# FFN up-projections by Strassen block products over both token halves, all of them ahead of the down-projections

## The chip, the cores and the metric

The kernel runs on one core of a Trainium2 chip. What is measured is the device time of one execution in microseconds (us), the median of several runs. The engines are named as in the profile: PE is the matrix engine (PEld its weight loads), DVE the vector engine, ACT the scalar engine, POOL GpSimd, and SP the engine whose queue issues nearly all DMAs. A matmul's result lies in a bank of PSUM; everything else lies in SBUF or in the chip's DRAM.

## The reference, cut to what matters

One block of a hybrid attention model on 1024 tokens with 1024 channels. The change touches the last line alone, the feed-forward part with its causal convolution of width 3 along the tokens:

```python
def _conv_ffn(h, w_up, conv_w, w_down):
    u = h @ w_up                                   # 1024 x 1024 @ 1024 x 5632
    u = lax.conv_general_dilated(u, conv_w[:, None, :], window_strides=(1,),
                                 padding=((CONV_WIDTH - 1, 0),), ...)
    a, b = jnp.split(u, 2, axis=-1)
    return (jax.nn.silu(a) * b) @ w_down           # 1024 x 2816 @ 2816 x 1024
...
        x = x + y @ w_out[l]
        x = x + _conv_ffn(_rms_norm(x, norm_ffn[l]), ffn_up[l], ffn_conv[l], ffn_down[l])
```

All of it is in float32, and the kernel keeps that accuracy: every matrix and every activation is split into a high part and a remainder ("hi" and "lo", e.g. whi and wlo), and one product is made of three matmuls, whi·xhi, whi·xlo and wlo·xhi, added in one PSUM bank.

## The kernel before

Channels lie on the 128 partitions, tokens along the free axis, in two halves h=0 and h=1 of 512. The 5632 up channels are 44 groups of 128; the gate pairs group i (o=0, called a) with group 22+i (o=1, called b), so that there are 22 **pairs** i. One up-projection of one group for one half is 8 k-tiles times 3 = 24 matmuls of a 128x128 weight tile by 128x512 tokens (`mm3`).

A weight group arrives by a DMA of 512 KB on SP's queue (`wraw`), ACT makes its hi part (L217), POOL its lo part (L218). The results are consumed from PSUM: ACT copies with the tap's factor (L1263), DVE adds the two other taps (L1267, which read PSUM and u) and the two leading tokens from the previous half (L1271: `prev`, 1 and 2 columns wide); ACT takes the tanh (L1278), DVE forms silu times gate (L1279, L1280), ACT and POOL split that into hh and hl (L1283, L1284).

Before the stretch of the change, half 0 of pairs 0 to 11 (NE = 12) is done as filler work, with results in DRAM (`th_d`) and the last two columns of its u in `cvl`. After the norm of half 1 the loop `for g0 in range(0, 22, GR)` runs over 11 groups of two pairs: their up-projections (half 1 alone for i < 12, both halves for i >= 12), then 96 matmuls of the down-projection with these two pairs (L1303), in PSUM banks P and B, which DVE adds to x2, the residual (L1305). After the last group every x2 tile of 512 KB is stored to the output. PSUM has two banks under each of the names P, M, A, B; up-projections use A (o=0) and M (o=1).

The order on each engine is set by a scheduler that moves work by priorities and expected times; on each engine instructions then run strictly in that order. The rows below show the order that came out. wload has two slots for each of its hi and lo tiles.

## Time and profile before

| | |
|---|---|
| median of 3 runs | 1878.68 us (1877.69 to 1880.37) |
| the profiled execution: its time / its span | 1885.57 us / 1883.8 us |
| PE busy | 1817.6 us, 96% of the span |
| DVE, ACT, POOL busy | 981.5 us (52%), 796.1 us (42%), 657.7 us (35%) |
| mean granted PE clock | 0.984 |

The span is the time from the first to the last instruction in the trace; the profiled execution's own time is 1.8 us more. Busy times are sums over each engine. A row of a timeline gives the start, the duration, the engine, the line and operation, out<-in, the shape, and in brackets how long the engine was idle just before and what it is thought to have waited for. In a table by windows the numbers in brackets count instructions.

### The profile page before, as it was taken

How to read it: one execution, taken by the hardware profiler on the slowest of the kernel's cores; microseconds unless marked ns; L12 is line 12 of the kernel's file. 1: busy time of each engine (PE TensorE's matmuls, PEld its weight loads, DVE VectorE, ACT ScalarE, POOL GpSimd, SP SyncE). 2: the span in 40 equal slices, each digit the busy share in tenths (PEclk: the TensorE clock that was granted, in tenths of full speed). 3: DMA queues.
4: the chain of work that ended last, by engine and by line, in shares of the span. 5: the costliest groups of instructions: out<-in, count | busy, mean ns of one | idle time of the engine just before them, and what ended most of it. 6: DMA issues, size and time to landing. Idle time of an engine off the chain costs nothing.

```text
span 1883.8 us, 30458 instructions
## 1 busy us (share of the span) xinstructions
PE 1817.6 (96%) x12106; PEld 1417.4 (75%) x12106; DVE 981.5 (52%) x1775; ACT 796.1 (42%) x1434; POOL 657.7 (35%) x412
## 2 busy tenths in 40 slices
PE   8999999999999999999999799989999999999998
PEld 5984657777777787777777588878888888888886
DVE  6213666768766504973453454256665553444443
ACT  5243665657556532454564444344222222212210
POOL 5222033141233334212155265656444433323320
...
GB/s 175 122 58 166 35 157 107 77 110 61 125 129 124 132 132 231 96 174 159 209 128 135 165 209 141 95 117 191 79 90 79 83 56 56 57 28 63 37 9 89
DMA packets 121342, 211.28 MB, mean 112 GB/s; under 512 B 23664, under 2 KB 52720, under 8 KB 120944
## 3 DMA queue, kind: packets, MB, share of 16 engines
...
q14 instruction: 47, 0.39, 0.1%
...
## 4 chain that ended last, share of the span: by engine, by line
PE 47%; DVE 2%; issue 2%; ACT 1%; DMA 1%; POOL 0%; POOLq 0%; SPq 0%; DVEq 0%
PE psA L224 11%; PE psP L224 10%; PE psM L224 9%; PE psP L1303 6%; PE psB L1303 6%; PE psB L224 1%; PE psA L1080 1%; DVE hf L204 0%; PE psM L999 0%; DMA zs<-x_d 0%; PE psB L1109 0%; PE psA L1096 0%; PE psM L943 0%; PE psC L1133 0%; DMA zs<-orw_d 0%
## 5 line engine op out<-in xcount | busy, mean ns | idle before, releaser
L218 POOL TENSOR_TENSOR wlo<-wraw,whi 128x1024 fp32r<-128x1024 f32 (+1 forms) x154 | 347.3, 2259 | 566.8 <-ACT whi L217 174.0
L224 PE MATMUL psP<-hhi,whi 128*128 128x512 f32 x816 | 333.4, 410 | 15.7 <-ACT hhi L704 9.3
L224 PE MATMUL psP<-hlo,whi 128*128 128x512 f32 x816 | 329.2, 404 | 4.2 <-DVE hlo L705 2.8
L217 ACT ACTIVATE whi<-wraw 128x1024 fp32r<-128x1024 f32 (+1 forms) x154 | 152.3, 990 | 209.0 <-PE psP L224 78.4
L224 PE MATMUL psP<-hhi,wlo 128*128 128x512 f32 x816 | 216.5, 399 | 0.0
L224 PEld LDWEIGHTS psP<-hhi,whi 128*128 128x128 f32 x816 | 156.0, 191 | 53.8 <-ACT hhi L704 11.0
L224 PEld LDWEIGHTS psP<-hlo,whi 128*128 128x128 f32 x816 | 156.1, 191 | 40.7 <-DVE hlo L705 4.2
L224 PEld LDWEIGHTS psP<-hhi,wlo 128*128 128x128 f32 x816 | 152.4, 190 | 33.3 <-issue 0.5
L541 DVE TENSOR_TENSOR pl<-pf,ph 128x512 f16<-128x512 f32 (+3 forms) x208 | 123.8, 604 | 44.6 <-ACT pf L540 43.7
L539 ACT ACTIVATE ph<-psA 128x512 f16<-128x512 f32 (+3 forms) x208 | 99.2, 477 | 62.0 <-PE psA L534 44.5
L482 DVE TENSOR_REDUCE mp<-psM 128x1 f32<-128x512 f32 (+1 forms) x192 | 94.5, 515 | 49.5 <-PE psM L480 42.4
L1290 POOL TENSOR_TENSOR dl<-draw,dh 128x1024 fp32r<-128x1024 f32 x22 | 53.6, 2455 | 156.0 <-ACT dh L1289 96.8
L1267 DVE SCALAR_TENSOR_TENSOR u<-psA,par,u 128x511 f32<-128x511 f32 x64 | 47.7, 746 | 100.1 <-ACT u L1263 99.8
L540 ACT ACTIVATE pf<-psA 128x512 f32<-128x512 f32 (+3 forms) x208 | 99.9, 480 | 0.0
L1305 DVE TENSOR_TENSOR x<-x,psP 128x512 f32<-128x512 f32 x88 | 60.3, 685 | 70.0 <-PE psP L1303 69.6
L1289 ACT ACTIVATE dh<-draw 128x1024 fp32r<-128x1024 f32 x22 | 22.3, 1054 | 151.9 <-PE psB L1303 148.2
L1305 DVE TENSOR_TENSOR x<-x,psB 128x512 f32<-128x512 f32 x88 | 60.3, 685 | 45.5 <-PE psB L1303 45.5
L1267 DVE SCALAR_TENSOR_TENSOR u<-psM,par,u 128x511 f32<-128x511 f32 x64 | 47.8, 746 | 63.7 <-ACT u L1263 63.4
L1284 POOL TENSOR_TENSOR hl<-th,hh 128x1024 fp32r<-128x1024 f32 x22 | 52.8, 2402 | 74.6 <-ACT hh L1283 74.6
L544 PEld LDWEIGHTS <-ph 128*128 128x128 f16 x592 | 55.7, 96 | 23.0 <-issue 12.3
L1303 PE MATMUL psP<-hh,dh 128*128 128x512 f32 x176 | 69.5, 395 | 2.1 <-ACT hh L1283 2.1
L549 PEld LDWEIGHTS <-pl 128*128 128x128 f16 x592 | 55.3, 98 | 20.6 <-issue 6.4
...
## 6 DMA issues: line engine op xcount, KB each, us to landing
wraw<-f_up SPq DMA_DIRECT2D x68, 512.0 KB, 3.4
wraw<-w_t SPq DMA_DIRECT2D x46, 512.0 KB, 3.7
draw<-f_dn SPq DMA_DIRECT2D x22, 512.0 KB, 3.3
sg_d<-zs SPq DMA_DIRECT2D x32, 256.0 KB, 2.0
wraw<-w_out SPq DMA_DIRECT2D x16, 512.0 KB, 3.3
z_d<-zs SPq DMA_DIRECT2D x28, 256.0 KB, 2.4
x<-xT SPq DMA_DIRECT2D x24, 256.0 KB, 5.9
zs<-sg_d SPq DMA_DIRECT2D x24, 256.0 KB, 3.0
```

The source lines that it names most:

```text
L217: A.activation(hi[:, :nk], raw, AF.Copy)
L218: G.tensor_sub(lo[:, :nk], raw, hi[:, :nk].bitcast(F32))
L224: T.matmul(ps, a[:, k], ks_(b, k), start=(n == 0), stop=(n == 3 * nk - 1))
L482: V.reduce_max(mp[:, x, br, t:t + 1], pm[:, 0:(b1 - b0) * 128], axis=AX.X)
L539: A.activation(ph[0:nkey, rg], pa[0:nkey, rg], AF.Exp, scale=0.125)
L540: A.activation(pf[0:nkey, rg], pa[0:nkey, rg], AF.Exp, scale=0.125)
L541: V.tensor_sub(pl[0:nkey, rg], pf[0:nkey, rg], ph[0:nkey, rg])
L544: T.matmul(pov[:, t, :], ph[0:nkey, tk], vt[0:nkey, kb, g, 0:65], start=first, stop=False, skip_group_check=True)
L549: T.matmul(pov[:, t, :], pl[0:nkey, tk], vt[0:nkey, kb, g, 0:65], start=False, stop=True, skip_group_check=True)
L1267: V.scalar_tensor_tensor(u[:, e0 + d:e0 + 512], pj[:, 0:512 - d], cw_, u[:, e0 + d:e0 + 512], op0=ALU.mult, op1=ALU.add)
L1303: T.matmul(pj, a[:, m], b[:, H[h]], start=(n == 0), stop=(n == 3 * len(hd_) - 1))
L1305: V.tensor_add(x2[m][:, H[h]], x2[m][:, H[h]], pj)
```

## The change

- **Order.** The loop over groups is taken apart into three phases. First the 24 up-projections of half 1 for i < 12, through four weight slots (`wslot`: whi, s12h, whi, s34h) with the weights of three groups prepared ahead (PFD = 3). Then pairs 12 to 21. Then all 11 down groups. The gate results th are stored to DRAM (`th_d`, now for both halves and all pairs) and reloaded for the down groups, x2 of half 1 goes to DRAM too (`x2_d[1]`, L1247) and both halves of x2 come back into `acc` tiles, in slots of activations that are no longer needed.
- **Strassen products.** For a pair i >= 12 the two weight groups, each cut into k-tiles 0-3 and 4-7, and the activations, cut into the same k halves and into the two token halves, form a 2x2 by 2x2 block product. It is made of 7 block products of 4 k-tiles (12 matmuls each, `prod`), 84 matmuls, where the loop before has 4 times 24 = 96. Called P1 to P7 in the order in which the code writes them: P1 and P3 in bank P (`pa`), P2, P5, P7 in bank M (`pb`), P4 and P6 in bank A (`pc`); bank B (`pd_`) receives a sum.
- **Sums that this takes.** Of activations, once: `tprep`, 12 DVE operations and 4 splits (ACT, DVE) for each of 4 k, spread over the first phase by `tsteps`. Of weights, for each pair: `prep_up`, four DVE operations of 128x512 (s12, s34) and splits of a, s12, s34 (128x1024 each) and of half of b. Of products, for each pair: p1 (ACT copies P1), u2 = P2 + p1, q = P4 + p1, PD = (P2+P5) + q, PC = (P4+P6) + u2, PB = (P2+P5+P7) + p1 on DVE, the last three written into PSUM. The tiles are accumulated in the same bank, so P5 comes after u2 has read the bank, P6 after q, P7 after PD.
- **Output** in 16 stores of 256 KB instead of 8 of 512 KB.

```diff
-            for i in ks:
-                uv = []
-                for o in range(2):
-                    ci = 22 * o + i
-                    hi, lo = wload(D["f_up"][ci], 8)
...
-                    for h in range(i < NE, 2):
-                        pj = ps("AM"[o])
-                        pu.append(pj)
-                        mm3(pj, hi, lo, h2hi[h], h2lo[h], 8)
...
-                A.activation(hh, th, AF.Copy)
-                G.tensor_sub(hl, th, hh.bitcast(F32))
...
+            for k in range(8):
+                nc.sync.dma_start(x2_d[1][k], x2[k])
...
+            f12, f22 = summed(1, k), summed(1, k + 4)
+            t3 = diff(3, f22, f12, "fu")
+            t1 = diff(1, f12, summed(0, k), "fu")
+            yield
+            split(3, t3)
+            split(1, t1)
+            t2 = diff(2, f22, t1, "fu")
+            t4 = diff(4, summed(0, k + 4), t2, "yx")
+            yield
+            split(2, t2)
+            split(4, t4)
...
+        wq = [wslot(D["f_up"][22 * (n % 2) + n // 2]) for n in range(PFD)]
+        for i in range(NE):
+            us = []
+            for o in range(2):
+                n = 2 * i + o + PFD
+                if n < 2 * NE:
+                    wq.append(wslot(D["f_up"][22 * (n % 2) + n // 2]))
+                hi, lo = wq.pop(0)
+                u = utile(o, 1)
+                pj = ps("AM"[o])
+                mm3(pj, hi, lo, h2hi[1], h2lo[1], 8)
+                taps(u, o, i, 1, pj, lambda d: cvl[:, i, o, 2 - d:2])
+                us.append(u)
+            t_ = silu(i, 1, *us)
+            with tc.issue_after(t_):
+                for k in tsteps[i]:
+                    next(tg[k])
...
+        def prep_up(i):
+            ra, rb = wraw(D["f_up"][i]), wraw(D["f_up"][22 + i])
+            w = {"a": split8(ra, wp, wp, "whi", "wlo", bufs=2)}
+            yield w
+            s12 = fp.tile([128, 8, 128], F32, name="s12")
+            V.tensor_add(s12[:, lo4], rb[:, lo4], rb[:, hi4])
+            V.tensor_sub(s12[:, hi4], s12[:, lo4], ra[:, lo4])
+            w["12"] = split8(s12, fp, fp, "s12h", "s12l")
+            yield
+            s34 = fp.tile([128, 8, 128], F32, name="s34")
+            V.tensor_sub(s34[:, lo4], ra[:, lo4], rb[:, lo4])
+            V.tensor_sub(s34[:, hi4], ra[:, hi4], s12[:, hi4])
+            w["34"] = split8(s34, fp, fp, "s34h", "s34l")
+            yield
+            w["b"] = split8(rb, wp, wp, "whi", "wlo", hi4, bufs=2)
+            yield
...
+        for i in range(NE, 22):
+            g_ = prep_up(i + 1) if i < 21 else iter([None] * 4)
+            pa, pb, pc, pd_ = ps("P"), ps("M"), ps("A"), ps("B")
+            prod(pa, w["a"], 0, b11, True)
+            p1 = tmp("p1", "zs", NZS)
+            A.activation(p1, pa, AF.Copy)
+            prod(pb, w["12"], 4, TB[2], True)
+            u2 = tmp("u2", "fu", 3)
+            V.tensor_add(u2, pb, p1)
+            prod(pa, w["a"], 4, b21, False)
+            wn = next(g_)
+            prod(pc, w["12"], 0, TB[1], True)
+            q = tmp("q", "fu", 3)
+            V.tensor_add(q, pc, p1)
+            next(g_)
+            prod(pb, w["34"], 0, TB[3], False)
+            V.tensor_add(pd_, pb, q)
+            u = [[utile(o, h) for h in range(2)] for o in range(2)]
+            taps(u[0][0], 0, i, 0, pa, None)
+            prod(pc, w["34"], 4, b22, False)
+            next(g_)
+            V.tensor_add(pc, pc, u2)
+            taps(u[0][1], 0, i, 1, pc, lambda d: pa[:, 512 - d:512])
+            prod(pb, w["b"], 4, TB[4], False)
+            next(g_)
+            V.tensor_add(pb, pb, p1)
+            taps(u[1][0], 1, i, 0, pb, None)
+            taps(u[1][1], 1, i, 1, pd_, lambda d: pb[:, 512 - d:512])
+            silu(i, 0, u[0][0], u[1][0])
+            silu(i, 1, u[0][1], u[1][1])
+            w = wn
...
+                    load(raw[:, h], th_d[h][i])
...
+                    A.activation(hi, raw[:, h], AF.Copy)
+                    G.tensor_sub(lo, raw[:, h], hi.bitcast(F32))
```

Up to the first up-projection matmul after the norm of half 1 the order of instructions is the same on every engine; from there PE has 2592 matmuls before (576 for half 1 of i < 12, 960 for i >= 12, 1056 down) and 2472 now (576, 840, 1056).

**DVE, third pair of the Strassen phase.** Before, where a pair i >= 12 is worked on: the last adds of a down group, the taps of b for both halves, the gate, and the taps of the next a.

```order
1545 L1305 TENSOR_TENSOR x_7_13375<-x_7_13375,psP 128x512
1546 L1305 TENSOR_TENSOR x_7_13375<-x_7_13375,psB 128x512
1547 L1267 SCALAR_TENSOR_TENSOR u_17018<-psM,par,u_17018 128x511
1548 L1267 SCALAR_TENSOR_TENSOR u_17018<-psM,par,u_17018 128x510
1549 L1267 SCALAR_TENSOR_TENSOR u_17018<-psM,par,u_17018 128x511
1550 L1271 SCALAR_TENSOR_TENSOR u_17018<-psM,par,u_17018 128x1
1551 L1267 SCALAR_TENSOR_TENSOR u_17018<-psM,par,u_17018 128x510
1552 L1271 SCALAR_TENSOR_TENSOR u_17018<-psM,par,u_17018 128x2
1553 L1280 SCALAR_TENSOR_TENSOR th<-th,u_17018 128x1024
1554 L1267 SCALAR_TENSOR_TENSOR u_17097<-psA,par,u_17097 128x511
```

Now, at pair i=14, from its u2 (row 1457: u_15734) to its PD (row 1466). u_15639 and u_15640 are of pair 13 (b, half 0 and half 1), u_15790 is pair 14's a of half 0, the L1271 rows are pair 13's last gate products.

```order
1457 L1402 TENSOR_TENSOR u_15734<-psM,p_15720 128x512
1458 L1262 SCALAR_TENSOR_TENSOR u_15639<-psM,par,u_15639 128x510
1459 L1264 SCALAR_TENSOR_TENSOR u_15640<-psM,par,u_15640 128x1
1460 L1271 SCALAR_TENSOR_TENSOR th<-th,u_15639 128x512
1461 L1264 SCALAR_TENSOR_TENSOR u_15640<-psM,par,u_15640 128x2
1462 L1271 SCALAR_TENSOR_TENSOR th<-th,u_15640 128x512
1463 L1262 SCALAR_TENSOR_TENSOR u_15790<-psP,par,u_15790 128x511
1464 L1262 SCALAR_TENSOR_TENSOR u_15790<-psP,par,u_15790 128x510
1465 L1407 TENSOR_TENSOR q<-psA,p_15720 128x512
1466 L1410 TENSOR_TENSOR psB<-psM,q 128x512
```

q stands behind both last gate products of the pair ahead and behind two taps. The order repeats every three pairs: at i = 14, 17, 20 it is this; at i = 13, 16, 19 q stands ahead of both gate products, and four operations on weights and taps stand between these and PD; at i = 12, 15, 18, 21 q stands behind the gate products, and the taps behind q.

**PE, the same place.** Before, products of 24 matmuls follow each other in banks A and M, with no wait on DVE inside a pair (the end of the last such product is in the next piece). Now, at i=14, the end of P1 of pair 15 (bank P) and the start of P6 of pair 14 (bank A), with the semaphores that a row waits for:

```order
10548 L1361 MATMUL psP<-hhi_12696,whi 128x512
10549 L1361 MATMUL psP<-hlo_12704,whi 128x512
10550 L1361 MATMUL psP<-hhi_12693,wlo 128x512 [waits Pool_49]
10551 L1361 MATMUL psP<-hhi_12694,wlo 128x512
10552 L1361 MATMUL psP<-hhi_12695,wlo 128x512
10553 L1361 MATMUL psA<-h2hi_13644,s34h 128x512 [waits DVE_49]
10554 L1361 MATMUL psA<-h2lo_13652,s34h 128x512
```

The products do not run in the order of the code: over three pairs PE's order is P1 P2 P4 P3 P5 of 12, 11 matmuls of P1 and P2 of 13, P6 P7 of 12, the rest of P1 and P2 of 13, P4 P3 P5 P6 of 13, P1 of 14, P7 of 13, P2 P3 P4 P5 of 14, 11 matmuls of P1 of 15, P6 P7 of 14, the last matmul of P1 of 15, and so on. The row with the wait for DVE is the one that needs q.

**PE, the last down group.** Before, from its seventh matmul; the waits of rows 11957 and 11961 are for hh and hl of the last pair, i=21.

```order
11953 L1303 MATMUL psP<-hh,dl 128x512
11954 L1303 MATMUL psB<-hh,dh 128x512
11955 L1303 MATMUL psB<-hl,dh 128x512
11956 L1303 MATMUL psB<-hh,dl 128x512
11957 L1303 MATMUL psP<-hh,dh 128x512 [waits Activation_49]
11958 L1303 MATMUL psB<-hh,dh 128x512
11959 L1303 MATMUL psP<-hh,dh 128x512
11960 L1303 MATMUL psB<-hh,dh 128x512
11961 L1303 MATMUL psP<-hl,dh 128x512 [waits Pool_49]
11962 L1303 MATMUL psP<-hh,dl 128x512
```

Now, the start of the last down group; its hh and hl are split from reloaded th, and ten down groups stand between these and the last gate product.

```order
12114 L1462 MATMUL psP<-hh,whi 128x512 [waits DVE_49,Activation_49]
12115 L1462 MATMUL psP<-hl,whi 128x512 [waits Pool_49]
12116 L1462 MATMUL psP<-hh,wlo 128x512
12117 L1462 MATMUL psP<-hh,s12h 128x512 [waits Activation_49]
12118 L1462 MATMUL psP<-hl,s12h 128x512 [waits Pool_49]
12119 L1462 MATMUL psP<-hh,s12l 128x512
12120 L1462 MATMUL psB<-hh,whi 128x512 [waits DVE_49]
```

The waits are in the same places, on tiles that are prepared while the group ahead of it runs.

## Rows read from the trace of the kernel before

**Rows 1.** The head of the page: the span, then busy time, share of the span and instructions of each engine.

```profile
span 1883.8 us, 30458 instructions
PE 1817.6 (96%) x12106; PEld 1417.4 (75%) x12106; DVE 981.5 (52%) x1775; ACT 796.1 (42%) x1434; POOL 657.7 (35%) x412
```

**Rows 2.** Windows of the span: from:to, length, busy time (and instructions) of PE, PEld, DVE, ACT, POOL, granted PE clock, share and GB/s of the DMA engines.

```profile
1200.00:1300.00 100.00, 94.98 (x404) 76.55 (x404) 48.39 (x55) 43.53 (x63) 63.12 (x30) 0.98 0.44 148
1300.00:1400.00 100.00, 100.00 (x439) 82.24 (x438) 60.09 (x83) 28.75 (x34) 45.29 (x20) 1.00 0.27 87
...
1700.00:1800.00 100.00, 100.00 (x439) 81.96 (x438) 41.71 (x65) 24.71 (x29) 28.80 (x12) 1.00 0.13 43
```

**Rows 3.** PE's timeline: the first up-projection matmul of the changed stretch, the twelfth matmul of the last down group and the two after it that waited, and the kernel's last matmul; then DVE's last row.

```profile
1280.09 0.40 PE L224 MATMUL psA<-h2hi,whi 128*128 128x512 f32 x1
...
1853.56 0.39 PE L1303 MATMUL psB<-hh,dl 128*128 128x512 f32 x1
1856.04 0.50 PE L1303 MATMUL psP<-hh,dh 128*128 128x512 f32 x1 [2.09 <-ACT hh L1283]
...
1858.48 0.80 PE L1303 MATMUL psP<-hl,dh 128*128 128x512 f32 x1 [1.24 <-POOL hl L1284]
...
1879.12 0.39 PE L1303 MATMUL psB<-hh,dl 128*128 128x512 f32 x1
...
1879.54 0.69 DVE L1305 TENSOR_TENSOR x<-x,psB 128x512 f32<-128x512 f32 x1 [0.67 <-PE psB L1303]
```

**Rows 4.** Timelines of DVE, ACT and POOL at the end of the last up-projection: the last gate product and its split.

```profile
1853.67 1.23 DVE L1280 SCALAR_TENSOR_TENSOR th<-th,u 128x1024 f32<-128x1024 f32 x1
1854.93 1.06 ACT L1283 ACTIVATE hh<-th 128x1024 fp32r<-128x1024 f32 x1 [2.99 <-DVE th L1280]
1856.06 2.36 POOL L1284 TENSOR_TENSOR hl<-th,hh 128x1024 fp32r<-128x1024 f32 x1 [19.56 <-ACT hh L1283]
```

**Rows 5.** DMA issues of the page: out<-in, count, KB each, median us from issue to landing; the last row is from the waits of SP's queue: what was waited for, us in total, times, longest.

```profile
out<-x SPq DMA_DIRECT2D x8, 512.0 KB, 2.6
th_d<-zs SPq DMA_DIRECT2D x12, 256.0 KB, 3.9
th<-th_d SPq DMA_DIRECT2D x12, 256.0 KB, 2.6
...
rk_d<-zr SPq DMA_DIRECT2D x8, 256.0 KB, 2.0
...
SPq L137 <- POOL wlo L218: 521.2, 124, 25.3
```

**Rows 6.** Groups of instructions between 1300 us and the end: count, busy time and mean ns of one, then the idle time ahead of them.

```profile
L218 POOL TENSOR_TENSOR wlo<-wraw,whi 128x1024 fp32r<-128x1024 f32 x38 | 91.4, 2406 | 140.8 <-PE psM L224 71.6 <-PE psA L224 44.5 <-ACT whi L217 24.6
...
L217 ACT ACTIVATE whi<-wraw 128x1024 fp32r<-128x1024 f32 x37 | 39.0, 1055 | 74.6 <-PE psA L224 40.6 <-PE psM L224 34.0
...
L1263 ACT ACTIVATE u<-psA,par 128x512 f32<-128x512 f32 x30 | 20.7, 689 | 33.9 <-PE psA L224 33.6
...
L1305 DVE TENSOR_TENSOR x<-x,psP 128x512 f32<-128x512 f32 x88 | 60.3, 685 | 70.0 <-PE psP L1303 69.6
L1271 DVE SCALAR_TENSOR_TENSOR u<-cvl,par,u 128x1 f32<-128x1 f32 x20 | 29.8, 1489 | 0.0
L1267 DVE SCALAR_TENSOR_TENSOR u<-psM,par,u 128x511 f32<-128x511 f32 x30 | 22.5, 750 | 61.1 <-ACT u L1263 61.1
...
L1271 DVE SCALAR_TENSOR_TENSOR u<-cvl,par,u 128x2 f32<-128x2 f32 x20 | 12.0, 601 | 0.0
L1279 DVE SCALAR_TENSOR_TENSOR th<-th,u 128x512 f32<-128x512 f32 x10 | 6.9, 692 | 8.1 <-ACT th L1278 8.1
...
L1271 DVE SCALAR_TENSOR_TENSOR u<-psM,par,u 128x1 f32<-128x1 f32 x10 | 2.1, 209 | 0.0
```

**Rows 7.** DVE's and POOL's timelines, 1341 to 1346 us: taps and leading tokens of an up-projection of half 1 with a pair i < 12, beside splits of weights.

```profile
1341.40 0.75 DVE L1267 SCALAR_TENSOR_TENSOR u<-psA,par,u 128x511 f32<-128x511 f32 x1 [2.16 <-ACT u L1263]
1342.06 1.53 DVE L1271 SCALAR_TENSOR_TENSOR u<-cvl,par,u 128x1 f32<-128x1 f32 x1
1343.51 0.74 DVE L1267 SCALAR_TENSOR_TENSOR u<-psA,par,u 128x510 f32<-128x510 f32 x1
1344.17 1.79 DVE L1271 SCALAR_TENSOR_TENSOR u<-cvl,par,u 128x2 f32<-128x2 f32 x1
...
1338.79 4.78 POOL L1290 TENSOR_TENSOR dl<-draw,dh 128x1024 fp32r<-128x1024 f32 x2 [11.84 <-PE psA L224]
1343.54 2.41 POOL L218 TENSOR_TENSOR wlo<-wraw,whi 128x1024 fp32r<-128x1024 f32 x1
```

**Rows 8.** Idle times of PE (timeline), and windows after idle times, with the granted clock in the third column from the right.

```profile
246.60 1.12 PE L823 MATMUL psP<-zg,lora 128*128 128x512 f32 x2 [1.67 <-ACT zs L829]
808.54 0.63 PE L943 MATMUL psM<-cst_f,zv 128*128 128x128 f32 x4 [1.69 <-issue]
...
246.70:250.70 4.00, 4.00 (x21) 1.72 (x22) 4.00 (x10) 2.61 (x8) 2.19 (x2) 1.00 0.38 113
420.30:423.60 3.30, 3.23 (x18) 2.41 (x19) 0.00 (x0) 1.79 (x4) 3.03 (x3) 0.50 0.20 75
809.40:816.10 6.70, 6.52 (x62) 4.79 (x63) 6.27 (x17) 6.19 (x13) 0.00 (x0) 0.50 0.38 116
1857.30:1864.00 6.70, 5.52 (x13) 4.38 (x14) 2.75 (x4) 0.00 (x0) 1.12 (x1) 0.50 0.22 88
```

More of the change, by code (lines that the diff above doesn't have):

```diff
@@ L244, in build @@
         np_d = [dr.tile([8, 128, 512], F32, name=f"np_d{h}") for h in range(2)]
[L245 to L246 removed]
+        x2_d = [dr.tile([8, 128, 512], F32, name=f"x2_d{h}") for h in range(2)]
+        th_d = [dr.tile([22, 128, 512], F32, name=f"th_d{h}") for h in range(2)]
         cvl = cp.tile([128, NE, 2, 2], F32, name="cvl")
@@ L1191, in build @@
         sqs = x2p.tile([128, 512], F32, name="sqs")
-        x2 = [x2p.tile([128, S], F32, name=f"x2_{k}") for k in range(8)]
+        x2 = [x2p.tile([128, 512], F32, name=f"x2_{k}") for k in range(8)]
         yst = ExitStack()
@@ L1246, in build, with taps @@
         yst.close()
+        x2st.close()
         fp = pool("ffn", 1, stack=fst)
+        def taps(u, o, i, h, pj, prev):
+            ci = 22 * o + i
+            A.activation(u, pj, AF.Copy, scale=P("conv", 88 + ci))
+            for d in (1, 2):
+                cw_ = P("conv", 44 * (2 - d) + ci)
+                V.scalar_tensor_tensor(u[:, d:512], pj[:, 0:512 - d], cw_, u[:, d:512], op0=ALU.mult, op1=ALU.add)
+                if h:
+                    V.scalar_tensor_tensor(u[:, 0:d], prev(d), cw_, u[:, 0:d], op0=ALU.mult, op1=ALU.add)
@@ new lines, in silu, with utile @@
+        def silu(i, h, ua, ub):
+            th = fp.tile([128, 512], F32, name="th", bufs=2)
+            with tc.issue_after(lasts[0]):
+                t_ = A.activation(th, ua, AF.Tanh, scale=0.5)
+            V.scalar_tensor_tensor(th, th, 1.0, ua, op0=ALU.add, op1=ALU.mult)
+            V.scalar_tensor_tensor(th, th, 0.5, ub, op0=ALU.mult, op1=ALU.mult)
+            nc.sync.dma_start(th_d[h][i], th)
+            return t_.ins
+        lasts = [None]
+        def utile(o, h):
+            return fp.tile([128, 512], F32, name=f"u{o}{h}", tag=f"u{o}{h}", bufs=(1, 2)[h])
@@ new lines, in build, with wraw, split8 @@
+        tg = [tprep(k) for k in range(4)]
+        tsteps = [(), (0,), (0,), (0, 1), (1,), (), (1, 2), (2,), (2, 3), (3,), (3,), ()]
+        rn_ = [1]
+        def wraw(src):
+            rn_[0] += 1
+            raw = (wp, fp)[rn_[0] // 2 % 2].tile([128, 8, 128], F32, name="wraw", bufs=2)
+            lastw[0] = load(raw, src).ins
+            return raw
+        def split8(raw, ph, pl, th, tl, ks=slice(0, 8), **kw):
+            hi = ph.tile([128, 8, 128], FR, name=th, **kw)
+            lo = pl.tile([128, 8, 128], FR, name=tl, **kw)
+            lasts[0] = A.activation(hi[:, ks], raw[:, ks], AF.Copy).ins
+            G.tensor_sub(lo[:, ks], raw[:, ks], hi[:, ks].bitcast(F32))
+            return hi, lo
@@ new lines, in prod @@
+        def prod(bank, w, o_, xs_, start):
+            n = 0
+            for k, wi, xi in [(k, 0, x_) for k in range(4) for x_ in (0, 1)] + [(k, 1, 0) for k in range(4)]:
+                T.matmul(bank, w[wi][:, o_ + k], xs_[k][xi], start=start and n == 0, stop=n == 11,
+                         skip_group_check=True)
+                n += 1
+        b11 = [(h2hi[0][k], h2lo[0][k]) for k in range(4)]
+        b21 = [(h2hi[0][k], h2lo[0][k]) for k in range(4, 8)]
+        b22 = [(h2hi[1][k], h2lo[1][k]) for k in range(4, 8)]
@@ new lines, in tmp @@
+        def tmp(name, tag, n):
+            return FP["f"].tile([128, 512], F32, name=name, tag=tag, bufs=n)
+        g_ = prep_up(NE)
+        w = next(g_)
+        for _ in range(3):
+            next(g_)
[23 more added lines that the diff above has]
+            prod(pb, w["b"], 4, TB[4], False)
+            next(g_)
+            V.tensor_add(pb, pb, p1)
[4 more added lines that the diff above has]
+            w = wn
@@ L1295, in build @@
                     for m in range(8):
-                        load(x2[m][:, H[0]], x2_d[m])
+                        for h in range(2):
+                            load(acc[m, h], x2_d[h][m])
             for m in range(8):
```

113 lines of the change are left out of this document (64 added, 49 removed).

## The prediction

> **What bounds the kernel now.** I read the page's head first: PE is busy for 96% of the span, the next engine for 52% [rows 1]. An average hides stages, so next the windows: from 1300 to 1800 us PE is busy for every us of every window at full clock, with 439 matmuls in 100 us, and DVE for 42 to 60 us [rows 2]. The change lies in this stretch, and there the number of matmuls is the time. The spacing comes from PE's timeline: the matmul at 1280.09 us is the first of the stretch's 2592 and the one at 1853.56 the 2508th (the last group has 96, this is its twelfth), so 573.47 / 2507 = **0.2287 us** for each [rows 3]. The same timeline shows the one place where PE stands still here: after 1853.56 it waits 2.09 us for hh and then 1.24 us for hl. What they wait for is one chain: the gate product on DVE ends at 1854.90, ACT's split at 1855.99, POOL's at 1858.42 [rows 4]; afterwards the clock is at half, 1.2 GHz, for 6.7 us [rows 8]. Behind the last matmul (1879.12) come one DVE add and the last store, until 1883.8 [rows 1, 3].
>
> **What the change takes away.** (1) Ten pairs times 12 matmuls: 120 x 0.2287 = **27.4 us**, if PE stays as dense; shape and banks' width stay as they are. (2) The end stall: from 1853.56 to 1879.12 PE has 84 matmuls, 19.2 us at full spacing, and takes 25.6. In the new order hh and hl of the last group are split while the group ahead runs (96 matmuls, 21.9 us, against four splits on ACT and some 10 us on POOL: 2 x 2.41 for the weights and four halves of about 1.3 [rows 6]), so **6.3 us** go. (3) The last store is half as large: 512 KB land in 2.6 us, other stores of 256 KB in 2.0 to 3.9 [rows 5]; I take **0.3**, with 0 to 0.6. Sum: 34.0 us.
>
> **What it adds, by phase.** *Half 1 of i < 12.* For each pair PE needs 48 x 0.2287 = 11.0 us. DVE: four taps at 0.66 from start to start, 2.6 [rows 7]; two leading tokens at 1.49 and two at 0.60, 4.2; two gate products, 1.2; 48 / 11 = 4.4 operations of tprep at 0.6, 2.6 [rows 6]. That is 10.6, so DVE keeps up, and two banks for A and two for M let it be late by a product. At worst the waits described below fill all of POOL's 4.8 us for each pair instead of the 3.3 in the 4.2: 12.1 against 11.0, 12 us over the phase, of which the banks absorb some 8. I take 0, with 0 to 4.
>
> *Strassen phase.* A pair is 84 matmuls, 19.2 us. DVE: five combinations at 0.6, eight taps at 0.66, four short ones at 0.2, four on weights and four on the gate at 0.6: 13.9 us. POOL: 3 x 2.41 + 1.3 = 8.5. Nobody is full. But PE runs in order, and P5, P6, P7 wait for u2, q, PD, so what counts is how late DVE is there. Here lies the question of this change, and rows 7 show it: the DVE row at 1342.06 is one column wide and lasts 1.53 us, till 1343.59, where POOL's split ends at 1343.57; the next one, 1.79, ends with POOL's next split (1345.95). The same line with one of its inputs in PSUM takes 0.21 [rows 6], and the taps between them, which also read PSUM, keep their 0.75. So a DVE operation with two SBUF inputs stands still while POOL's subtraction runs. In the new phase those are the eight on weights and gate.
>
> The Trainium skill, "SBUF — State Buffer", section "Who interferes with whom", says so as a rule: a DVE instruction with two SBUF inputs contends with a GpSimd instruction that reads SBUF, for its whole length, and PE and ACT wait for nobody. It speaks against this change; the trace agrees (1.53 against 0.21 us). With it the phase has the stalls worked out next; without it none of them, and the time would be that of the first rival.
>
> I step the order with these durations, 0.42 us from a last matmul's start to its reader [rows 3], 0.05 to 0.1 from engine to engine [rows 3, 4]. **At i = 14, 17, 20:** let 0 be the first matmul of P4. P3's end frees whi at 0.2; ACT splits a of the next pair until 1.25, POOL from 1.3 to 3.7. DVE, which has PB, two gate operations, two taps and u2 ahead, comes to the gate's last product for half 0 at about 2, is held until 3.7 and ends at 4.3. P4's end (2.9) lets ACT split s12 until 4.0; POOL takes it from 4.3 to 6.7, ahead of DVE, which first had a short one; the second gate product ends at 7.3. Two taps and q: 7.3 + 1.3 + 0.7 = 9.3, at PE 9.4. P6 is due behind P4, P5 and 11 matmuls of P1: 35 x 0.2287 = 8.0. **PE waits 1.4 us, three times: 4.2 us.** An idle of 1.67 us left the clock at 2.4 GHz, one of 1.69 was followed by 6.7 us at 1.2 GHz [rows 8]; 1.4 stays below. **At i = 13, 16, 19**, with 0 at P5's first matmul, the gate product is held until 4.6, then two on weights 1.2, two taps 1.3, PD 0.7: 7.9 with the hop; P7 is due after P5, P6 and P1: 36 matmuls, 8.2. It fits, with 0.3 to spare. At i = 12, 15, 18, 21 it is some 0.5.
>
> No row of before shows DVE writing PSUM here. Bounds: the same as reading it, 0.69, or two passes, 1.37 [rows 6]; I take the first, the nearest row. By the second the spare times go negative by 0.4 and 0.2: 3 x 0.4 + 4 x 0.2 = 2 us more.
>
> *Into the down phase.* P4's end in pair 21 leaves 36 matmuls, 8.2 us, in which POOL makes two weight splits, 4.8, and hl, 4 x 1.3, most of which can start earlier; none of it late, at worst 10.0 - 8.2 = 1.8. Then 1056 matmuls, in which DVE, POOL and ACT have the same work for each pair as before or less. *DMA:* some 80 more transfers of 256 KB, 20 MB in 570 us, 36 GB/s beside 43 to 87, where 148 ran at 1200 to 1300 us [rows 2]. On SP's queue the eight x2 stores stand each ahead of a weight load that waits for POOL to free a slot, as SP's loads did 124 times [rows 5]: nothing.
>
> **Sum.** 34.0 - 4.2 = 29.8 us. Against the profiled span: 1883.8 - 29.8 = 1854.0. The profiled execution took 1885.57, 6.9 above the median of the runs; I carry over the difference: 1878.68 - 29.8 = **1849 us**, 1.6% faster.
>
> **The rivals.** *A, no waits:* POOL's splits fall between DVE's operations, since ACT, which releases them, is a little earlier or later than I step it. For it: POOL is busy for 8.5 of 19.2 us only; against: at i = 14 two splits follow so closely that DVE meets both. 1878.68 - 34.0 = 1844.7.
>
> *B, the waits pass the clock's limit:* ACT and DVE work some 5 to 10% longer at i = 14, 17, 20 makes the wait 1.7 to 1.9, and each brings a stretch at half clock, 3.3 or 6.7 us long [rows 8], of which half is lost: 3 x (1.8 + 1.65 to 3.35) = 10 to 15, and PD's waits up to 3: 1855 to 1863; with losses in the first phase to 1867. For it: only 0.3 us lie between 1.4 and the limit.
>
> *C, the other side:* q or PD late by 1.7 us in every pair, not in three of ten. The place is P6 or P7 in each pair; POOL's split of s12 or a always starts just ahead of the gate products. Price: ten times 1.7 + 1.65 = 33.5, no change (1878); with the longer stretches 10 x 5.05 = 50, 1895. It decides at 3.4 us lost for each pair. For it: these two kinds of work meet in every pair; against: at three of ten q stands ahead of both gate products, and at four P4 and P3 end nearly together, so that ACT frees POOL's splits some 5 us later, when DVE has the gate behind it.
>
> *D, the end stall comes back* at the first down group, as 4 us or so with a fall of the clock: 1855; I count it with B.
>
> **Chances.** The forecast, 1846.5 to 1853: 0.42. A: 0.20. B with D: 0.21. C: 0.17, of which two fifths end within 0.2% (3.8 us, about what a measurement of this kernel can tell from no change) and the rest above. So faster 0.82, same 0.07, slower 0.11. The range runs from A less 1.7 us, 1843, to B's end with 1 us over it, 1868; it leaves out C and little more.
>
> **What would show it.** In the trace after: 12 matmuls fewer for each pair; no idle ahead of the last down group; about 1854 us of span; from some 1412 to 1608 us the seven products, with idle of about 1.4 us named as waits for DVE's q ahead of bank A's matmuls at three places, next to gate products on DVE of 1.5 to 3 us that end just after a POOL split; and full clock throughout. Waits for q of 1.7 us and more with clock 0.50 behind them mean B, the same in each pair C, none A. Idle in bank A or M before 1412 would mean that tprep does not fit. Wrong at the root would be a spacing other than 0.2287 inside the products.

## The result, and the profile after

The changed kernel took **1859.87 us**, the median of six runs (1852.62 to 1866.02), the kernel before beside it 1879.06 (1877.69 to 1884.56): ratio 0.9889, 95% interval 0.9861 to 0.9917, 19.2 us faster. In two later comparisons it was 1855.01 beside 1877.87 (0.9873, 0.9858 to 0.9889) and 1856.35 beside 1878.68 (0.9898, 0.9881 to 0.9914). So 19 to 23 us were gained where 29.8 were forecast. The times lie in the stated range, 6 to 11 us above the stated value. Two executions of variants lie far outside all others, one of e1_classic (2090.84 us, mean granted clock 0.804) and one of e11_hf3 (9877.84 us); no trace of either was kept, and the figures below leave them out.

The head of the page answers to [rows 1]: 120 matmuls fewer on PE, and 119 us more work on DVE.

```profile
span 1850.8 us, 30936 instructions
PE 1786.8 (97%) x11986; PEld 1389.8 (75%) x11986; DVE 1100.7 (59%) x1933; ACT 824.4 (45%) x1512; POOL 706.2 (38%) x454
```

Windows, as [rows 2]. The first phase runs to about 1406 us, the Strassen products to 1604, then the down groups.

```profile
1300.00:1400.00 100.00, 98.22 (x427) 79.54 (x426) 92.77 (x123) 37.06 (x55) 46.05 (x18) 1.00 0.33 111
1400.00:1500.00 100.00, 97.17 (x422) 78.58 (x421) 86.56 (x129) 41.60 (x58) 45.76 (x21) 1.00 0.23 79
1500.00:1600.00 100.00, 99.60 (x435) 81.18 (x434) 87.68 (x126) 45.49 (x65) 49.93 (x25) 1.00 0.39 132
...
1700.00:1800.00 100.00, 100.00 (x432) 80.89 (x431) 49.19 (x73) 16.82 (x24) 39.21 (x24) 1.00 0.26 84
```

Three things to see. DVE, 60 us of 100 before, is now busy for 87 to 93 until 1600 us. PE has holes until 1600, so DVE has come next to it as a limit. And from 1700 to 1800 PE has no hole and full clock, yet runs 432 matmuls where 439 ran before: they stand wider apart.

PE's timeline, the ends of the changed stretch as in [rows 3]: the first up-projection matmul in bank A, and the last matmul.

```profile
1272.17 0.40 PE L225 MATMUL psA<-h2hi,whi 128*128 128x512 f32 x1
...
1846.79 0.40 PE L1462 MATMUL psP<-hh,s12l 128*128 128x512 f32 x1
```

That is 574.6 us; seven matmuls of the second product now run ahead of this first one, among the filler work, 1.6 us more: 576.2 against 599.0. **The changed stretch gained 22.8 us**, the tail behind the last matmul (4.65 us, now 4.05) 0.6. PE's waits in the stretch, the five largest of seven rows (us in total, times, longest):

```profile
PE psP L1361 <- ACT p L1399: 1.3, 1, 1.3
PE psM L1361 <- DVE u L1402: 1.1, 1, 1.1
PE psM L225 <- DVE u L1264: 0.9, 1, 0.9
PE psA L1361 <- DVE q L1407: 0.6, 3, 0.2
PE psA L225 <- DVE u L1264: 0.6, 1, 0.6
```

The view counts the engine's idle time; after each wait the first two matmuls are also wider apart (0.31 to 0.34 us instead of 0.23), so a wait costs about 0.3 us more than its row. Counted as spacing above 0.228 us between starts, the waits cost 7.7 us: 2.9 in the first phase, 3.4 at the start of the products (1407 to 1420 us), 1.4 for q. The rest, (574.6 - 7.7) / 2464 = 0.2301 us for each matmul, stands against 0.2287 before.

**Stretches rather than medians.** Ahead of the change, where both kernels do the same, the granted clock drops to 0.50, 1.2 GHz, for 3 to 24 us at a time, at places and for lengths that differ from one execution to the next (in the trace after, for 6.8 us from 1239.4, in and behind a wait of 3.9 us that ends at 1240.3); in the traces the stretch begins anywhere from 1270 to 1286 us. The medians carry this; the stretch does not, since it has full clock throughout but for 6.8 us behind the end stall of the kernel before. The table gives it for each trace (but those of the two tries at the spacing, further down), with matmuls that run ahead of its first one added at 0.228 us. The expectations quoted below count it without these: 574.5 there is 576.1 here.

Single spans mislead in the same way. Those of the two profiled executions, 1883.8 and 1850.8, differ by 33.0 us, more than was forecast, but 9.5 of it lies ahead of the change: the stretch starts at 1280.09 us before and, with its seven early matmuls, at 1270.6 us after.

| kernel | stretch us | cost of waits in it us | us for each other matmul |
|---|---|---|---|
| before, two traces | 599.0, 598.5 | 6.5, 5.9 (end stall) | 0.2287 |
| changed, three traces | 576.2, 576.1, 576.1 | 7.7 | 0.2300 to 0.2301 |
| e1_classic | 591.8 | 0 | 0.2284 |
| e2_no_tprep | 573.2 | 3.9 | 0.2304 |
| e3_no_lo | 571.4 | 3.3 | 0.2299 |
| e5_act_lead | 576.6 | 8.2 | 0.2300 |
| e9_hf, e10_hf_act | 569.8, 569.7 | 1.5, 1.4 | 0.2300 |
| e11_hf3 | 571.0 | 2.7 | 0.2300 |

### The profile page after: what moved, and what is told of

Its sections match the earlier page's. It is cut to its first block, busy times and chain, and to the rows that moved or that the text cites. A ratio compares the mean times of both kernels' runs of the same rounds, so it can differ in the third digit from the quotient of the medians.

```text
span 1850.8 us, 30936 instructions
## 1 busy us (share of the span) xinstructions
PE 1786.8 (97%) x11986; PEld 1389.8 (75%) x11986; DVE 1100.7 (59%) x1933; ACT 824.4 (45%) x1512; POOL 706.2 (38%) x454
## 5 line engine op out<-in xcount | busy, mean ns | idle before, releaser
L219 POOL TENSOR_TENSOR wlo<-wraw,whi 128x1024 fp32r<-128x1024 f32 (+1 forms) x110 | 241.2, 2197 | 419.8 <-ACT whi L218 147.5
L218 ACT ACTIVATE whi<-wraw 128x1024 fp32r<-128x1024 f32 (+1 forms) x110 | 106.0, 964 | 130.0 <-PE psP L225 79.9
L1328 POOL TENSOR_TENSOR wlo<-wraw,whi 128x1024 fp32r<-128x1024 f32 (+1 forms) x43 | 99.0, 2302 | 44.9 <-ACT whi L1327 32.6
L1446 POOL TENSOR_TENSOR hl<-thr,hh 128x512 fp32r<-128x512 f32 x44 | 57.9, 1329 | 114.8 <-ACT hh L1445 114.8
L1445 ACT ACTIVATE hh<-thr 128x512 fp32r<-128x512 f32 x44 | 27.2, 625 | 163.9 <-PE psB L1462 160.3
L1464 DVE TENSOR_TENSOR acc<-acc,psP 128x512 f32<-128x512 f32 x88 | 60.5, 687 | 59.3 <-PE psP L1462 59.3
L1464 DVE TENSOR_TENSOR acc<-acc,psB 128x512 f32<-128x512 f32 x88 | 60.5, 687 | 59.3 <-PE psB L1462 59.3
L564 POOL TENSOR_TENSOR onat<-onat,ot 128x256 f32<-128x256 f32 x32 | 25.0, 783 | 111.8 <-DVE ot L563 88.8
L720 DVE SCALAR_TENSOR_TENSOR fu<-psP,par,fu 128x511 f32<-128x511 f32 (+1 forms) x48 | 35.8, 747 | 41.1 <-ACT cvl L718 40.4
L1269 ACT ACTIVATE th<-u 128x512 f32<-128x512 f32 x32 | 20.1, 627 | 84.8 <-issue 70.5
```

Source lines behind the costliest of these rows:

```text
L218: A.activation(hi[:, :nk], raw, AF.Copy)
L219: G.tensor_sub(lo[:, :nk], raw, hi[:, :nk].bitcast(F32))
L1328: G.tensor_sub(lo[:, ks], raw[:, ks], hi[:, ks].bitcast(F32))
L1446: G.tensor_sub(lo, raw[:, h], hi.bitcast(F32))
L1464: V.tensor_add(acc[m, h], acc[m, h], pj)
```

## The experiments

**Where the missing us are: in the stretch or in the head.** The changed kernel and the kernel before were run again.

> The changed kernel once more, unaltered. Its runs so far lie between 1852.6 and 1866.0 us, those of the kernel before between 1877.7 and 1884.6. Theory S: the slower runs lose their time in the new phases, where PE idles of 1.3 and 1.5 us (at 1414 and 1419 us of the first trace) are near the 1.7 that brings the clock down; then a trace of a slow run has a stretch of clock 0.50 between 1270 and 1450 us, and the first up-projection of half 1 starts at about 1272 us as before. Rival H: the slower runs lose it ahead of the change, by the falls of the clock that the kernel before has too; then the first up-projection starts up to 13 us later and the stretch behind it lasts 574.6 us (first to last matmul) as in the first trace. Median by both 1855 to 1863.

> The kernel before once more, unaltered, for a second trace. Theory H (the traces differ ahead of the change): the stretch from the first up-projection of half 1 to the last matmul lasts 599.0 us again, with the same end stall of 6.4 us, while its start lies between 1271 and 1281 us (1280.1 in the first trace). Rival: the stretch itself varies by several us from run to run, and the comparison of single traces with it.

The changed kernel's stretch came out within 0.1 us of the first trace, that of before within 0.6. The start moved instead: 1272.2, 1274.6 and 1275.2 us for the changed kernel, 1280.1 and 1276.4 for before. So in the traces what the change did is 22.8 + 0.6 = 23.4 us, and the traces differ by the head alone. That the slower executions of the first comparison, up to 1866.02 us, lost their time in the head too is likely but not shown: no execution of the changed kernel above 1855.51 us was traced. Their mean granted clock was lower (0.983 at 1866.02, 0.989 at 1852.62 us); where it fell is not known.

**The order alone.** Pairs 12 to 21 as four products of 24 matmuls, no tprep, everything else in the new order:

```diff
         for i in range(NE, 22):
-            prod(pa, w["a"], 0, b11, True)
...
+            for o in range(2):
...
+                for h in range(2):
+                    mm3(pj, hi, lo, h2hi[h], h2lo[h], 8)
+                    taps(u, o, i, h, pj, lambda d: pu[0][:, 512 - d:512])
```

> The new order alone: all up-projections ahead of all down-projections, th and x2 through DRAM, but pairs 12 to 21 by four products of 24 matmuls as before, and no sums of activations or weights. Theory (the prediction's terms): the end stall and the smaller store go, 6.6 us, the 120 matmuls stay; 1872, or 1875 if the matmuls of the down phase follow each other at 0.2322 us here too, as they do in the trace after (0.2290 before). No idle of PE between the first up-projection of half 1 and the last matmul. Rival: most of the gain comes from the order; then 1860 to 1866. By theory S its runs scatter as little as those before (3 us), by rival H as those after (13 us).

1868.58 us, the median of five (1866.81 to 1872.96), ratio 0.9957 (0.9941 to 0.9972). The trace has no wait at all in the stretch. The ends of the stretch (twelve matmuls run ahead of it), and a window that is as dense as before:

```profile
1271.99 0.40 PE L225 MATMUL psA<-h2hi,whi 128*128 128x512 f32 x1
...
1861.01 0.39 PE L1373 MATMUL psB<-hh,s12l 128*128 128x512 f32 x1
```

```profile
1700.00:1800.00 100.00, 100.00 (x441) 82.43 (x440) 50.36 (x74) 21.01 (x30) 44.76 (x28) 1.00 0.27 85
```

So the order gives 599.0 - 591.8 = 7.2 us where 6.6 were expected, the end stall and a little; the products add 15.6 of their 27.4: 7.7 go back in waits, the rest, 4.1, in wider spacing.

**Without the sums of activations.** The products read h2hi and h2lo where T1 to T4 would stand, and tprep is not run; the matmuls stay the same in number and shape:

```diff
+        TB[1], TB[2], TB[3], TB[4] = b11, b21, b22, b21
...
-            with tc.issue_after(t_):
-                for k in tsteps[i]:
-                    next(tg[k])
```

> The changed kernel without tprep: the products take the unsummed activations in place of T1 to T4, 48 sums and 16 splits on DVE and 16 on ACT are left out of the first phase (the output is another one). Theory: DVE, which was late from tprep, keeps up, and the waits of PE ahead of banks A and M between 1341 and 1394 us (2.8 us in all) go, and most of the 3.1 us at 1407 to 1419 us, where DVE was still behind; the stretch from the first up-projection to the last matmul falls from 574.6 to 568 to 570 us. Rival: these waits come from POOL's splits alone, and 2 us or more of them stay ahead of 1408 us.

1851.2 us, ratio 0.9867 (0.9848 to 0.9886). What is left out is 48 operations on DVE (32 sums and differences, 16 splits) and 16 on ACT; the expectation counts 48 sums. The windows show DVE freed and PE full. Its list of waits has only two rows, at the start of the down phase (those for q, 0.12 to 0.14 us each, are too short for it):

```profile
1300.00:1400.00 100.00, 100.00 (x441) 82.45 (x440) 65.44 (x100) 35.94 (x46) 44.15 (x19) 1.00 0.32 114
```

```profile
PE psB L1426 <- DVE acc L1428: 1.3, 1, 1.3
PE psP L1426 <- DVE u L1264: 0.4, 1, 0.4
```

All 6.3 us before 1420 us are gone: tprep's load makes them, the three at the start of the products too. Without the matmuls ahead of it the stretch took 571.6 us, more than the 568 to 570 expected: 2.7 us are lost at the start of the down phase, where the changed kernel waits for nothing.

**Without POOL's splits in the products.** The lo tile of a weight is its hi tile, so that POOL has no subtraction there:

```diff
-            lo = pl.tile([128, 8, 128], FR, name=tl, **kw)
+            lo = hi if nolo[0] else pl.tile([128, 8, 128], FR, name=tl, **kw)
...
+            if nolo[0]:
+                return hi, hi
```

> The changed kernel without POOL's subtractions in the Strassen phase: the hi part of the weights is used in place of the lo part (the output is another one). PE has as many matmuls. Theory (DVE's operations with two inputs in SBUF stand still while POOL subtracts): no row of the gate or of the weights on DVE is longer than 0.75 us between 1420 and 1600 us, and the waits for q at i = 14, 17, 20 (0.46 us each in the trace after) go; the waits of the first phase (2.8 us) stay. Stretch from the first up-projection to the last matmul 571 to 573 us. Rival: the rows stay long without POOL, since DVE waits there for something else; then the stretch stays at 574.

1849.54 us, ratio 0.9851 (0.9834 to 0.9869). The q waits and those at the start of the products are gone, the first phase keeps its 2.9, and 0.4 us appear at the first down group. So the waits at the start of the products need both, the backlog of the first phase (e2_no_tprep) and POOL's splits of the first pairs' weights (here): with the backlog and without these splits there are none. Groups of DVE's instructions from 1420 to 1600 us, first of the changed kernel, then of this one (busy us, mean ns):

```profile
L1271 DVE SCALAR_TENSOR_TENSOR th<-th,u 128x512 f32<-128x512 f32 x18 | 36.9, 2050 | 0.3
L1270 DVE SCALAR_TENSOR_TENSOR th<-th,u 128x512 f32<-128x512 f32 x19 | 13.0, 723 | 1.2 <-ACT th L1269 1.2
L1380 DVE TENSOR_TENSOR s<-wraw 128x512 f32<-128x512 f32 x8 | 9.9, 1235 | 0.0
```

```profile
L1271 DVE SCALAR_TENSOR_TENSOR th<-th,u 128x512 f32<-128x512 f32 x18 | 13.7, 764 | 0.2
...
L1384 DVE TENSOR_TENSOR s<-wraw 128x512 f32<-128x512 f32 x8 | 5.5, 692 | 2.8 <-ACT s34h L1329 2.8
```

The same instruction takes 2.05 us beside POOL's splits and 0.76 without them: the contention on which the prediction rested is shown by taking its cause away. (Three rows of DVE from 1586 us on still take 1.06 to 2.92 us; by then POOL makes the splits for the down phase, which were left in.) L1270 beside it, of the same form, is at 0.72 in the changed kernel; which of them meets a split is a matter of the place in the order.

**Relief for DVE, first try.** The leading tokens of the first phase as small ACT operations:

```diff
+            if cv is not None:
+                for c, d in ((0, 1), (0, 2), (1, 2)):
+                    s_ = 2 - d + c
+                    A.activation(u[:, c:c + 1], cv[:, s_:s_ + 1], AF.Identity, ...)
```

> The changed kernel with one thing moved: in the first phase the leading tokens from cvl (four DVE operations for each pair, 0.69 and 0.52 us on average because they stand still beside POOL) are added by ACT, six operations of one column with the tap as scale and u as bias. Theory (DVE, full from 1327 to 1419 us, is late by more than two banks hold): DVE gets some 2.4 us for each pair back, the waits of PE ahead of 1400 us (2.8 us) and at 1408 to 1419 us (3.4 us) go, and the stretch from first up-projection to last matmul falls from 574.5 to 568 to 570 us; the median falls by 4 to 6 us. Rival: ACT's longer chain (three operations ahead of the first tap of each product, 0.6 us) makes DVE wait as long as it saves; then the waits stay at 5 us or more and the stretch at 573 or above.

1859.13 us, ratio 0.9873 (0.9843 to 0.9903), waits 8.2 us: no gain, the rival's outcome. Part of the stalls passed to the next operations with two SBUF inputs. Groups from 1285 to 1420 us of this kernel, then the last one as it was in the changed kernel:

```profile
L1277 DVE SCALAR_TENSOR_TENSOR th<-th,u 128x512 f32<-128x512 f32 x11 | 13.9, 1264 | 1.0
L1291 DVE TENSOR_TENSOR zs<-hhi,hlo 128x512 f32<-128x512 f32 x8 | 12.7, 1588 | 2.3 <-DMA th_d<-zs 2.2
```

```profile
L1285 DVE TENSOR_TENSOR zs<-hhi,hlo 128x512 f32<-128x512 f32 x7 | 4.8, 679 | 0.0
```

So some of what the leading tokens stood still beside POOL is now stood still by others of their kind. Not all: DVE's busy share from 1300 to 1400 us fell from 92.8 to 88.3, and still PE waited as long. The rival's own reason, the three operations of ACT ahead of each first tap, is not separated from this here; in e10_hf_act below, the same three operations cost PE no wait.

**Two tries at the wider spacing.** The accumulators of the down phase in other tiles (as e1_classic has them), and PE moved on by one small matmul:

```diff
-                    acc[m, h] = hp2.tile([128, 512], F32, ..., tag=f"{('h2hi', 'h2lo')[h]}_{m}")
+                    acc[m, h] = fp.tile([128, 512], F32, ..., tag=f"T4{'hl'[h]}{m}")
```

> The changed kernel with half of the accumulators of the down phase in the slots of T4 and not in those of h2 (where the kernel e1_classic has them too). Question: the down phase's matmuls follow each other at 0.2322 us in the changed kernel and at 0.2278 in e1_classic, with the same instructions. Theory A: it is where the accumulators lie, which DVE reads and writes beside PE; then 0.2278. Theory B: something else; then 0.2322. In either case some 2 to 4 us of wait at the start of the phase, since T4 comes free only with the last product, and x2 is loaded behind that.

```diff
+            if g0 == 2:
+                pn = ps("A")
+                T.matmul(pn[:, 0:128], wd_[0][0][:, 0], hd_[0][0][0][:, 0:128], start=True, stop=True)
```

> The changed kernel with one more matmul of 128 columns, whose result nobody reads, ahead of the third down group. Question as for e6_acc. Theory C: the spacing is a matter of the phase in which PE's instructions follow one another, and a shift changes it; then 0.2322 in the first two groups and another value behind the extra matmul. Theory B: placement or program; then 0.2322 throughout.

The mean spacing in the down phase stayed at 0.2322 us in both. e6_acc, one run of 1870.15 with a late start (1286.2), paid 3.7 us of waiting at the first down group for its accumulators; e7_nudge took 1854.33. The extra matmul ran at 1608.99 us, inside the first down group and not ahead of the third. It did move which spacings are wide (from 1700 to 1800 us 0.229 us behind hl by whi in the changed kernel, 0.236 here; 0.233 and 0.226 behind hh by s12l), but not their mean. So neither the place of half the accumulators nor a shift by one matmul explains the mean; the places of hh, hl and the weights were not moved.

**Relief for DVE, second try.** tprep needs the normed half 1, which it sums again from hi and lo; here it is stored to DRAM when it is made and loaded back, eight sums of sixteen fewer:

```diff
-                hf = tp_.tile([128, 512], F32, name="hf", bufs=3)
+                hf = tp_.tile([128, 512], F32, name="hf", bufs=8)
...
+                nc.sync.dma_start(hf_d[k], hfs[k])
...
-            f12, f22 = summed(1, k), summed(1, k + 4)
+            f12, f22 = hfl[k], hfl[k + 4]
...
+                load(hfl[kk], hf_d[kk])
```

> The changed kernel with 8 of tprep's 16 sums hi + lo left away: the normed half 1, which these sums make again, is stored to DRAM at its norm (8 stores of 256 KB) and loaded into the slots of T4 (8 loads). DVE has 8 operations with two SBUF inputs less in the first phase (1.42 us each on average in the trace after). Theory (what DVE cannot do beside POOL in the first phase is carried on as lateness up to 1419 us): the waits of PE up to 1397 us (2.8 us) fall below 1 us and those at 1408 to 1419 us (3.4 us) below 2; stretch from first up-projection to last matmul 570 to 572 us (574.5 after). Rival: as with the leading tokens on ACT, DVE's other operations meet POOL's subtractions in place of those taken away, and the stretch stays at 574 or above.

> Both changes of e5_act_lead and e9_hf together. Theory: the two reliefs of DVE add up; no wait of PE ahead of 1400 us and below 1 us at 1408 to 1419 us; stretch 568 to 570 us. Rival: ACT's three small operations ahead of the taps hold them back as in e5_act_lead, whose waits were 6.7 us up to 1421 us; stretch 572 us or more.

The stretch fell to 569.8 us with little but q's waits left (1.4 of 1.5 us), yet the medians did not: 1860.33 us (0.9889, 0.9867 to 0.9912), and 1856.41 (0.9883, 0.9855 to 0.991) for e10_hf_act, which moves the leading tokens to ACT besides. The loss lies ahead of the stretch. DVE's timeline of e9_hf, and the row of PE's waits:

```profile
1231.91 9.58 DVE L1245 SCALAR_TENSOR_TENSOR hf<-x,par,rstd 128x512 f32<-128x512 f32 x8 [3.25 <-ACT rstd L197]
1241.42 2.83 DVE L1248 TENSOR_TENSOR h2lo<-hf,h2hi 128x512 fp32r<-128x512 f32 x1
1244.17 0.74 DVE L721 SCALAR_TENSOR_TENSOR fu<-psP,par,fu 128x511 f32<-128x511 f32 x1
```

```profile
PE psP L225 <- DVE fu L721: 11.9, 1, 11.9
```

With eight buffers in place of three, all eight scalings went ahead of the taps for which the filler's PE work waits; the changed kernel loses 3.9 us there. The last pair of runs puts the scalings back between the taps and keeps the stores.

```diff
+                    if k > 2:
+                        hs.enter_context(tc.issue_after(hls[k - 2 if k - 3 in NPOOL else k - 3]))
                     V.scalar_tensor_tensor(hf, x2[k], P("norm_ffn", k), rstd[:, H[1]], ...)
```

> As e9_hf (the normed half 1 is stored to DRAM and loaded back, so that tprep makes 8 sums instead of 16), but the eight scalings that make it stand on DVE between the taps of the filler work, in about the order of the changed kernel, instead of all ahead of them. e9_hf's trace shows both sides: its changed stretch took 568.2 us instead of 574.5, with no wait before 1460 us, and ahead of it PE waited 11.9 us for DVE's fu near 1240 us, where the changed kernel waits 3.9. Theory 'only the order cost it': that wait is 4 to 5 us here, the stretch stays at 568 to 569, and the median comes out 5 to 7 us under e12_again, at 0.983 to 0.986 of the kernel before. Rival 'the transfers cost it' (2 MB out and 2 MB back on SP's queue, ahead of weight loads): PE still idles some 12 us near 1240, or the first weights of the stretch come late, and the median is that of e12_again.

> The changed kernel once more, beside e11_hf3 on one chip: 1852 to 1860 us, stretch 574.5 us with 7.7 us of waits in the trace.

**e11_hf3 took 1846.8 us**, the median of four between 1845.95 and 1853.91, against 1856.35 (1855.51 to 1862.2) for the changed kernel and 1878.68 for before on the same chip: ratio 0.9843, 0.9824 to 0.9862. It beats both; the interval of the changed kernel beside it is 0.9881 to 0.9914. Its windows and its waits in the stretch:

```profile
1300.00:1400.00 100.00, 100.00 (x441) 82.44 (x440) 91.35 (x125) 41.58 (x61) 45.18 (x19) 1.00 0.33 114
1400.00:1500.00 100.00, 99.81 (x437) 81.63 (x437) 87.03 (x129) 40.45 (x56) 44.69 (x21) 1.00 0.22 80
```

```profile
PE psA L1375 <- DVE q L1421: 0.9, 3, 0.5
PE psB L1476 <- DVE acc L1478: 0.7, 1, 0.7
```

The stretch, 571.0 against 576.1 us, explains 5.1 of the 9.5 us between the two; the rest is the head, where the profiled runs differ by 3.6 us with other drops of the clock. It still waits 5.2 us up to 1240.3 us, where 4 to 5 were expected, now for ACT's h2hi.

## Why the prediction came out as it did

**Right.** *120 matmuls*, *the end stall* (6.3 forecast, 6.5 measured, none left), *the last store* (0.3; the tail lost 0.6). *No drop of the clock in the stretch*, so rivals B, C and D did not come, and A, with no waits, did not either; nothing waits at the first down group. *DVE writing PSUM*, taken as 0.69 us, took 0.69 to 0.70 (L1410, L1415, L1419). *The contention of DVE and POOL*, settled by e3_no_lo, and the page of the Trainium skill that states it, "SBUF — State Buffer", section "Who interferes with whom", agrees with the traces: 2.05 us against 0.76.

*The place of the q waits* was right, three and no more, at i = 14, 17, 20. Timeline of PE, ACT, POOL and DVE at i = 14, from P3's last reader of whi to P6:

```profile
1453.78 0.39 PE L1361 MATMUL psP<-hlo,whi 128*128 128x512 f32 x1
1454.00 1.07 PE L1361 MATMUL psP<-hhi,wlo 128*128 128x512 f32 x4
1454.91 0.39 PE L1361 MATMUL psA<-T1h,s12h 128*128 128x512 f32 x1
...
1454.25 1.06 ACT L1327 ACTIVATE whi<-wraw 128x1024 fp32r<-128x1024 f32 x1 [0.71 <-PE psP L1361]
...
1455.39 2.40 POOL L1328 TENSOR_TENSOR wlo<-wraw,whi 128x1024 fp32r<-128x1024 f32 x1 [4.34 <-ACT whi L1327]
...
1455.97 2.37 DVE L1271 SCALAR_TENSOR_TENSOR th<-th,u 128x512 f32<-128x512 f32 x1
...
1458.09 2.51 POOL L1328 TENSOR_TENSOR s12l<-s,s12h 128x1024 fp32r<-128x1024 f32 x1 [0.30 <-ACT s12h L1327]
...
1458.51 2.64 DVE L1271 SCALAR_TENSOR_TENSOR th<-th,u 128x512 f32<-128x512 f32 x1
...
1462.51 0.68 DVE L1407 TENSOR_TENSOR q<-psA,p 128x512 f32<-128x512 f32 x1
...
1463.25 0.50 PE L1361 MATMUL psA<-h2hi,s34h 128*128 128x512 f32 x1 [0.19 <-DVE q L1407]
```

This is the chain as it was stepped: POOL split, gate product held to its end, the next split, the next gate product, taps, q.

**Right by luck.** The forecast's own bracket was 1846.5 to 1853 us, and all three medians miss it. They lie where rival B had its time, 1855 to 1863, by other causes than B's; the stated range held because it had been drawn to take in B.

B's price is not borne out either. It rests on two idle times, 1.67 and 1.69 us, between which the clock was taken to fall. In e5_act_lead PE stood still for 2.46 us at the start of the products and the granted clock stayed at 2.4 GHz, as it did in e6_acc behind 3.41 us; PE's timeline and a window of e5_act_lead:

```profile
1420.97 0.50 PE L1367 MATMUL psP<-hhi,whi 128*128 128x512 f32 x1 [2.46 <-ACT p L1405]
```

```profile
1421.00:1428.00 7.00, 7.00 (x31) 5.67 (x32) 5.93 (x9) 2.52 (x4) 3.99 (x3) 1.00 0.14 46
```

So the length of one idle time does not tell whether the clock falls (the expectation of e0_again leans on the same 1.7 us), and "1.4 stays below" came true without being shown to be the reason.

**Mis-sized, the q term (4.2, measured 1.4).** The step "P3's end frees whi at 0.2" is wrong: the last four of a product's 12 matmuls read wlo only, so whi is free after the eighth, four matmuls (0.9 us) earlier. ACT starts at 1454.25, 0.7 us ahead of P4's first matmul (1454.91) and not 0.2 behind it. The step "P4's end (2.9) lets ACT split s12" has the same error: ACT starts there at 1456.95, 2.0 on that scale. q is done at 8.3 instead of 9.3, P6 is due at 8.0 as forecast, and each wait costs 0.46 us instead of 1.4.

**Mis-sized, the first phase (0 with 0 to 4, measured 2.9).** DVE's sum for a pair, 10.6 us of 11.0, is near what was measured (busy 92.8 of 100), but by luck: the leading tokens took 28.3 us over the twelve pairs, 2.4 for each instead of 4.2, and tprep's 48 operations 54.1 us, 4.9 for each of eleven pairs instead of 2.6, since they are held beside POOL too. And the sum has no term for DVE's idle time ahead of nearly each first gate product, 0.75 us until ACT's tanh is done. The group from 1285 to 1407 us:

```profile
L1270 DVE SCALAR_TENSOR_TENSOR th<-th,u 128x512 f32<-128x512 f32 x11 | 7.6, 691 | 7.5 <-ACT th L1269 7.5
```

With it DVE has no time to spare, so the step "DVE keeps up" fails; and two banks of each name, which were to "let it be late by a product", stand against a load that is not even, since tprep's steps come in lumps. DVE's and POOL's timelines:

```profile
1334.00 3.50 DVE L1297 TENSOR_TENSOR t<-zs 128x512 f32<-128x512 f32 x2
1337.43 0.74 DVE L1262 SCALAR_TENSOR_TENSOR u<-psM,par,u 128x511 f32<-128x511 f32 x1
1338.09 1.69 DVE L1264 SCALAR_TENSOR_TENSOR u<-cvl,par,u 128x1 f32<-128x1 f32 x1
...
1334.23 2.73 POOL L1328 TENSOR_TENSOR s12l<-wraw,s12h 128x1024 fp32r<-128x1024 f32 x1 [7.81 <-ACT s12h L1327]
1336.92 2.85 POOL L1328 TENSOR_TENSOR wlo<-wraw,whi 128x1024 fp32r<-128x1024 f32 x1
```

**Missed, the start of the products (3.4).** The sum stepped the products as they repeat and never the first pair, where DVE is still behind from the first phase and meets POOL's splits of the first pairs' weights. ACT's and PE's timelines:

```profile
1411.84 0.63 ACT L1269 ACTIVATE th<-u 128x512 f32<-128x512 f32 x1 [5.56 <-issue]
1412.37 1.04 ACT L1327 ACTIVATE s34h<-s 128x1024 fp32r<-128x1024 f32 x1
1413.32 0.67 ACT L1259 ACTIVATE u<-psM,par 128x512 f32<-128x512 f32 x1
1413.89 0.59 ACT L1399 ACTIVATE p<-psP 128x512 f32<-128x512 f32 x1
...
1414.53 0.50 PE L1361 MATMUL psP<-hhi,whi 128*128 128x512 f32 x1 [1.34 <-ACT p L1399]
```

p1 of the first pair stands on ACT behind the tanh of pair 11, which waits for DVE's late taps; PE's P3 waits for p1, P5 then for u2.

**Mis-sized, the spacing (3.4).** "If PE stays as dense": inside the products it does (0.2285 to 0.2287 us from 1470 to 1570), in the down phase it is 0.2322 instead of 0.2287, 1056 x 0.0035 = 3.7 us, of which the first phase, a little closer than forecast, gives some back. Nothing in the rows of before showed it, and its cause stays open.

The sum with the measured terms: 27.4 + 6.5 + 0.6 - 1.4 - 2.9 - 3.4 - 3.4 = 23.4 us, against 29.8. The two errors on what DVE does in the first phase and just behind it are as large as the whole shortfall; that is a coincidence of sizes, since the error on q (2.8, in the change's favour) offsets most of the spacing.
